# Gather, prefix sum and matmul: three engines' unrolled streams become loops of 16 tiles with waits on counted registers

## The chip, the cores and the metric

The kernel runs on one NeuronCore of a Trainium2 chip. The metric is the device time of one execution in microseconds (us), as a median over several executions. A core has TensorE (PE: matmuls, with its weight loads shown as PEld), VectorE (DVE), ScalarE (ACT), GpSimd (POOL) and SyncE (SP), each running its own stream of instructions in order, and 16 DMA engines that move data between the DRAM and the on-chip SBUF. Engines wait for each other by semaphores: counters that an instruction raises when it ends and that others wait on. PE writes into PSUM[...], which VectorE and ScalarE read.

## The reference

For each of 16 batches, 2048 rows of 512 floats are picked from 4096 by sorted indices, their running sum along the rows is taken, and the result is multiplied by a 512 x 512 matrix.

```python
def reference(x, indices, w):
    B, S, D = x.shape                      # 16, 4096, 512
    N = indices.shape[1]                   # 2048
    b_idx = np.arange(B)[:, None]
    gathered = x[b_idx, indices, :].copy()
    cs = np.cumsum(gathered, axis=1)
    return np.matmul(cs, w).astype(np.float32)
```

## The kernel before

The work is cut into T = 256 tiles of 128 gathered rows, 16 tiles (NT) to a batch; two tiles (R = 2) make a group, the unit of storing. A tile goes through these steps, each on its own engine:

- `gather` (line 126, GpSimd): an indirect DMA brings 128 rows of 2 KB into one of 16 slots (NG) of `g32`. The gather of tile t waits until the pair of tiles that had its slots is cast (line 119).
- `cast` (line 141, ScalarE): float32 to float16 into `g16`, for one tile or for a pair at once.
- `sums` (line 152, PE): four matmuls with a triangle of ones (`ut`, or `uq` in the first and last group) give the running sums inside a tile, transposed, in one of four PSUM buffers `pa` (NA).
- `carry` (lines 171 and 184, VectorE): adds the last column of the tile before, and writes float16 to `cst`; the first tile of a batch is only copied. It waits for the sums of its tile and for its own carry before.
- `project` (line 195, PE): four matmuls with `w16` into one of four PSUM buffers `pb` (NB). Except in the first and last group it needs the carries of both tiles of its group.
- `drain` (line 207, ScalarE): copies `pb` to the output buffer `ob`.
- `store` (lines 216 and 221, SyncE): one DMA of 512 KB for a group, two of 256 KB in the first and last.

The order is written out by hand, one long unrolled stream for each engine, and set by a plan that is made in Python:

- ScalarE's stream (line 342) has, for each tile u, the casts of the list `casts[u]` and then the drain of u. The list (lines 106 to 114) keeps casts `far` tiles ahead of the drain: `far` grows from 2 to FAR = 10 with u // 8 and shrinks at the end with (T - 1 - u) // 6. Casts come in pairs while `far` is over 4.
- PE's stream (lines 319 to 334) sets sums of later tiles ahead of the project of tile u by `lead`: it grows from 1 to LEAD = 4 with u // 8 and shrinks at the end with (T - 1 - u) // 6. Inside a group of four matmuls it waits ahead for what the next group of matmuls needs (lines 150 and 193).
- VectorE's stream is carry after carry, GpSimd's is gather after gather, SyncE's is store after store.

All waits go through `Lane.need(sem, value)` (line 21), which leaves out a wait for a value that the engine has already waited for. Values are constants, since every tile has its own place in the unrolled stream. Most waits ride on the instruction that follows; where an instruction needs more of them, a wait instruction of its own stands ahead of it.

Before the first tile, small index loads (`idx_first`, line 229) serve the gathers of tiles 0 to 3. SyncE then issues two of the four loads of w (line 238, ScalarE the other two) and then the two loads of all indices (line 240). VectorE turns the indices to float (line 298), PE transposes them (line 303), and VectorE writes them back as `idxg` (line 309), which gathers from tile 4 on wait for. PE runs matmuls on zeros to stay warm: `busy(9)` ahead of the transposes and `busy(12)` behind them (lines 291, 299, 306). VectorE and ScalarE cast w to float16 (lines 312 and 341).

## Time and profile before

| what | value |
|---|---|
| median of 9 runs | 351.09 us (350.52 to 352.36) |
| the profiled execution | 351.98 us |
| its span in the profile | 350.3 us |
| PE busy, instructions | 307.8 us (88%), 2071 matmuls |
| ScalarE busy | 264.2 us (75%), 408 |
| GpSimd busy | 244.0 us (70%), 266 |
| VectorE busy | 179.1 us (51%), 263 |
| DMA | 135.91 MB, mean 388 GB/s |

The span begins with the first instruction of the program and ends with the last; the rest of the execution's time lies around it. The profile has a page (busy times, 40 slices of the span, DMA queues, the chain of work that ended last, groups of instructions by line) and views of the trace: waits, instructions in order of time, sums by stage. In a row of a group, `L126 POOL DMA_INDIRECT g<-in_x_dram,idxg x252 | 238.5, 946 | ...` means: line 126, GpSimd, 252 instructions of that kind, 238.5 us busy, 946 ns for one, and behind the second bar the idle time of the engine just ahead of them and what ended it. In a row in order of time the first number is the start and the second the duration, both in us; the brackets hold the idle time before. Registers, branches and waits are not counted as busy. PE's matmuls overlap, and their ends are modelled, so its busy share says little on how close it is to its limit. Queue q0 carries the gathers, q1 the stores, q8 and q14 the instructions that the engines themselves fetch.

### The profile page before, as it was taken

The numbers are of one execution on the slowest core, as the hardware profiler recorded it, in microseconds if no ns is written. First come the engines' busy times: TensorE is split into PE (matmuls) and PEld (weight loads), VectorE is DVE, ScalarE is ACT, GpSimd is POOL, SyncE is SP. The second block draws the span as 40 slices with busy tenths as digits, with TensorE's granted clock in tenths as the row PEclk, the third lists the DMA queues.
The fourth block names the chain that finished last, engine by engine and source line by source line (L and its number), as shares of the span: only waits on it lengthen the run. The fifth ranks groups of instructions, "written<-read, shape, count | busy, mean of one in ns | idle before, by whom it ended". The sixth has DMA issues, their size and how long they took to land.

```text
span 350.3 us, 5668 instructions
## 1 busy us (share of the span) xinstructions
PE 307.8 (88%) x2071; PEld 154.6 (44%) x2071; DVE 179.1 (51%) x263; ACT 264.2 (75%) x408; POOL 244.0 (70%) x266
## 2 busy tenths in 40 slices
PE   5878888999988899898999989889898989988984
PEld 2334443554444444454444445444454445544431
DVE  1335554565544555464555545555555556654441
ACT  3358876987687788787777778777777878877883
POOL 6777777777777777777777777777777777777000
PEclk9999999999999999999999999999999999999998
DMA  7699999999999999999999999999999999999974
GB/s 236 197 325 343 382 395 405 384 392 410 412 407 401 412 408 413 415 411 415 412 416 415 412 414 411 414 412 415 414 412 415 413 414 411 415 416 414 416 314 185
DMA packets 40635, 135.91 MB, mean 388 GB/s; under 512 B 6816, under 2 KB 7072, under 8 KB 40608
## 3 DMA queue, kind: packets, MB, share of 16 engines
q0 software_dynamic: 20480, 67.13, 49.7%
q1 hardware_dynamic: 19568, 67.91, 48.2%
q10 hardware_dynamic: 560, 0.53, 0.5%
q8 instruction: 16, 0.26, 0.3%
q14 instruction: 11, 0.09, 0.1%
HBM read 68.42 MB, written 67.11 MB: 387 GB/s over the span
## 4 chain that ended last, share of the span: by engine, by line
POOL 40%; DMA 17%; issue 16%; PE 14%; ACT 10%; DVE 1%; SPq 0%; ACTq 0%
POOL g L126 40%; DMA g<-in_x_dram,idxg 16%; PE pb L195 9%; ACT g L141 7%; PE pa L152 3%; ACT ob L207 3%; PE pb L291 1%; DMA idx<-in_indices_dram 1%; DVE cst L184 1%; SPq L238 0%; PE pb L303 0%; DVE cst L171 0%; SPq L229 0%; ACTq L23 0%; DVE idxf L298 0%
## 5 line engine op out<-in xcount | busy, mean ns | idle before, releaser
L126 POOL DMA_INDIRECT g<-in_x_dram,idxg x252 | 238.5, 946 | 77.1 <-issue 72.2
L195 PE MATMUL pb<-w,cst 128*128 128x512 f16 x1024 | 262.5, 379 | 3.8 <-DVE cst L184 3.1
L184 DVE TENSOR_TENSOR cst<-pa,cst 128x512 f16<-128x512 f32 x240 | 166.1, 692 | 141.1 <-PE pa L152 141.0
L141 ACT CAST g<-g 128x1024 f16<-128x1024 f32 (+1 forms) x148 | 137.6, 931 | 54.5 <-DMA g<-in_x_dram,idxg 51.8
L207 ACT COPY ob<-pb 128x512 f32<-128x512 f32 x256 | 139.9, 585 | 24.8 <-PE pb L195 24.8
L152 PE MATMUL pa<-ut,g 128*128 128x128 f16 x1008 | 110.4, 220 | 30.6 <-ACT ob L207 20.0
L152 PEld LDWEIGHTS pa<-ut,g 128*128 128x128 f16 x1008 | 71.1, 98 | 113.7 <-ACT ob L207 45.4
L195 PEld LDWEIGHTS pb<-w,cst 128*128 128x128 f16 x1024 | 89.3, 98 | 66.5 <-DVE cst L184 3.8
L171 DVE CAST cst<-pa 128x512 f16<-128x512 f32 x16 | 11.1, 692 | 17.2 <-PE pa L152 17.2
L291 PE MATMUL pb<-zeros 128*128 128x512 f16 x21 | 9.3, 633 | 1.5 <-DVE zeros L295 1.5
L291 PEld LDWEIGHTS pb<-zeros 128*128 128x128 f16 x21 | 3.1, 150 | 6.2 <-issue 4.7
L126 POOL DMA_INDIRECT g<-in_x_dram,idx_first x4 | 4.0, 993 | 1.6 <-issue 0.9
L298 DVE CAST idxf<-idx 128x128 f32<-128x128 uint32 x2 | 0.5, 228 | 5.9 <-DMA idx<-in_indices_dram 5.8
L338 ACT ACT_TABLE_LOAD x1 | 1.3, 1283 | 2.5 <-issue 2.5
L303 PE MATMUL pb<-ident,idxf 128*128 128x128 f32 x2 | 0.7, 460 | 2.1 <-DVE idxf L298 2.1
L152 PEld LDWEIGHTS pa<-uq,g 128*128 128x128 f16 x16 | 1.3, 112 | 1.4 <-ACT g L141 0.6
L303 PEld LDWEIGHTS pb<-ident,idxf 128*128 128x128 f32 x2 | 0.4, 181 | 3.1 <-issue 3.0
L152 PE MATMUL pa<-uq,g 128*128 128x128 f16 x16 | 1.6, 238 | 0.1
L341 ACT CAST w<-w 128x512 f16<-128x512 f32 x2 | 1.1, 616 | 0.5 <-DMA w<-in_w_dram 0.5
L295 DVE MEMSET zeros<- 128x256 uint32 x1 | 0.3, 272 | 1.1 <-SPq L82 1.1
L312 DVE CAST w<-w 128x512 f16<-128x512 f32 x2 | 0.8, 419 | 0.0
L309 DVE CAST idxg<-pb 128x128 uint32<-128x128 f32 x2 | 0.6, 292 | 0.3 <-PE pb L303 0.3
(11 smaller groups left out, 2.1 us busy)
## 6 DMA issues: line engine op xcount, KB each, us to landing
out_dram<-ob SPq DMA_DIRECT2D x126, 512.0 KB, 7.5
g<-in_x_dram,idxg POOLq DMA_INDIRECT x252, 9.3
out_dram<-ob SPq DMA_DIRECT2D x4, 256.0 KB, 2.7
w<-in_w_dram ACTq DMA_DIRECT2D x2, 256.0 KB, 4.1
w<-in_w_dram SPq DMA_DIRECT2D x2, 256.0 KB, 3.6
idx<-in_indices_dram SPq DMA_DIRECT2D x2, 128.0 KB, 4.6
g<-in_x_dram,idx_first POOLq DMA_INDIRECT x4, 3.6
idx_first<-in_indices_dram ACTq DMA_DIRECT2D x1, 2.0 KB, 2.1
```

Source lines behind the costliest of these rows:

```text
L126: nc.gpsimd.indirect_dma_start(out=g32[g % (NG // R)][:, r, :], out_offset=None, in_=x_flat, in_offset=bass.IndirectOffsetOnAxis(ap=ap, ax ...
L141: nc.scalar.copy(out=g16[g % NH][:, r : r + n], in_=g32[g % (NG // R)][:, r : r + n]).then_inc(s_c, 1)
L152: mm = nc.tensor.matmul(out=pa[t % NA][:, c], lhsT=g16[g % NH][:, r, c * P : (c + 1) * P], rhs=uq[:] if g in PLAIN else ut[:], start=(c == 0),
L171: nc.vector.tensor_copy(out=dst, in_=src).then_inc(s_d, 1)
L184: nc.vector.tensor_tensor(out=dst, in0=src, in1=last, op=mybir.AluOpType.add).then_inc(s_d, 1)
L195: mm = nc.tensor.matmul(out=pb[u % NB][:], lhsT=cst[g % NC][:, c, j, :], rhs=w16[:, c, :], start=(c == 0), stop=(c == DC - 1),)
L207: nc.scalar.copy(out=ob[g % NO][:, j], in_=pb[u % NB][:]).then_inc(s_e, 1)
L291: nc.tensor.matmul(out=pb[NB - 1][:], lhsT=zeros[:, :P], rhs=zeros[:], start=True, stop=True)
L303: nc.tensor.transpose(out=pb[k % NB][:, :P], in_=idxf[:, k, :], identity=ident[:]).then_inc(s_pt, 1)
L312: nc.vector.tensor_copy(out=w16[:, c, :], in_=w32[:, c, :]).then_inc(s_wc, 1)
L338: nc.scalar.copy(out=spare[:], in_=zeros[:, :1])
L341: nc.scalar.copy(out=w16[:, c, :], in_=w32[:, c, :]).then_inc(s_wc, 1)
```

## The change

The middle of three streams becomes a loop whose body is 16 tiles (U = NT) with an engine register as the count.

- VectorE: tiles 0 to 15 and 240 to 255 stay unrolled; 14 passes in between. The register `first` holds the first tile of the pass.
- PE: the plan up to the project of tile 31 and behind that of tile 223 stays unrolled; 12 passes in between. The register counts groups; tile counts are R times the register.
- ScalarE: tiles 0 to 31 and 224 to 255 stay unrolled; 12 passes.

`need` gets a `base`: inside a loop it waits for base + value, where base is the register, and remembers per pass what was waited for. At the head of each pass that memory is cleared. GpSimd and SyncE stay unrolled.

For every pass to be the same, the plan must be steady inside the loops. `far` now grows with u // 4 and shrinks with (T - 1 - u) // 4, so that it is 10 from tile 32 to tile 223 (before: 64 to 207). `lead` now grows with (u + 2) // 4; its end is as it was. Assertions check that the plan repeats.

Two edits stand apart from the loops: SyncE's two loads of all indices go ahead of the loads of w, and `busy(12)` becomes `busy(7)`.

```diff
-    def need(self, sem, value):
-        if value > 0 and self.seen.get(sem.num, 0) < value:
-            self.eng.wait_ge(sem, value)
-            self.seen[sem.num] = value
+    def need(self, sem, value, base=None):
+
+        seen = self.seen if base is None else self.in_pass
+        if base is None and value <= 0 or sem.num in seen and seen[sem.num] >= value:
+            return
+        self.eng.wait_ge(sem, value if base is None else base + value if value else base)
+        seen[sem.num] = value
+
+    def new_pass(self):
+        self.in_pass = {}
...
+    U = NT
...
-        far = min(FAR, 2 + u // 8, 2 + (T - 1 - u) // 6)
+        far = min(FAR, 2 + u // 4, 2 + (T - 1 - u) // 4)
...
-    def cast(t, n):
+    def cast(t, n, first=None):
         g, r = divmod(t, R)
         for u in range(t, t + n):
-            act.need(s_g[u % NG], 16 * (u // NG + 1))
+            act.need(s_g[u % NG], 16 * (u // NG + 1), first)
...
-    def sums(t, u):
+    def sums(t, u, first=None):
         g, r = divmod(t, R)
-        pe.need(s_c, cast_by[t])
-        pe.need(s_d, t - NA + 1)
+        tiles = None if first is None else R * first
+        pe.need(s_c, cast_by[t] if first is None else cast_by[2 * U + t] - 2 * U // R, first)
+        pe.need(s_d, t - NA + 1, tiles)
         for c in range(DC):
             if c == 1 and u is not None:
-                pe.need(s_e, u - NB + 1)
+                pe.need(s_e, u - NB + 1, tiles)
...
-    for c in range(DC):
-        eng = (nc.sync, nc.scalar)[c % 2]
-        eng.dma_start(out=w32[:, c, :], in_=w[c * P : (c + 1) * P, :]).then_inc(s_w[c], 16)
     for k in range(KI):
         nc.sync.dma_start(
             out=idx64[:, k, :], in_=idx_rows[k * P : (k + 1) * P, :]
         ).then_inc(s_idx[k], 16)
+    for c in range(DC):
+        eng = (nc.sync, nc.scalar)[c % 2]
+        eng.dma_start(out=w32[:, c, :], in_=w[c * P : (c + 1) * P, :]).then_inc(s_w[c], 16)
...
-    busy(12)
+    busy(7)
...
-    for t in range(T):
+    for t in range(U):
+        carry(t)
+    with nc.vector.Fori(U, T - U, U) as first:
+        dve.new_pass()
+        for t in range(U):
+            carry(t, first)
+    for t in range(T - U, T):
         carry(t)
...
-        lead = min(LEAD, 1 + u // 8, 1 + (T - 1 - u) // 6)
+        lead = min(LEAD, 1 + (u + 2) // 4, 1 + (T - 1 - u) // 6)
...
+    head = order.index((False, 2 * U - 1)) + 1
+    tail = order.index((False, T - 2 * U - 1)) + 1
+    step = 2 * U
...
+    for i in range(head):
+        run(i)
+    with nc.tensor.Fori(2 * U // R, (T - 2 * U) // R, U // R) as first:
+        pe.new_pass()
+        for i in range(head, head + step):
+            run(i, first)
+    for i in range(tail, len(order)):
+        run(i)
...
+    for u in range(2 * U):
+        step(u)
+    with nc.scalar.Fori(2 * U, T - 2 * U, U) as first:
+        act.new_pass()
+        for u in range(U):
+            step(u, first)
+    for u in range(T - 2 * U, T):
+        step(u)
```

`carry`, `project` and `drain` take `first` in the same way. `run` on PE calls `sums` or `project` for an entry of the plan, `step` on ScalarE is the old loop body for one tile.

## The prediction

> **What bounds the kernel now.** I read the slices first, then the groups, the waits, single tiles, and last the chain's end. Slices (clock, DMA busy share, GB/s in 40 slices) and queues:

> ```profile
> DMA  7699999999999999999999999999999999999974
> GB/s 236 197 325 343 382 395 405 384 392 410 412 407 401 412 408 413 415 411 415 412 416 415 412 414 411 414 412 415 414 412 415 413 414 411 415 416 414 416 314 185
> ...
> q8 instruction: 16, 0.26, 0.3%
> q14 instruction: 11, 0.09, 0.1%
> ```

> From about 60 us to 330 us the DMA engines are full at some 413 GB/s. They are half empty only in the first 20 us and the last 20. Instruction code is 0.35 MB.

> ```profile
> L126 POOL DMA_INDIRECT g<-in_x_dram,idxg x252 | 238.5, 946 | 77.1 <-issue 72.2
> L195 PE MATMUL pb<-w,cst 128*128 128x512 f16 x1024 | 262.5, 379 | 3.8 <-DVE cst L184 3.1
> ```

> GpSimd spends 946 ns on a gather and 0.3 us before the next: one per 1.25 us, never held, the last issued at 322.6 us. At 0.5 MB per tile (0.25 gathered, 0.25 stored) that asks for 419 GB/s, a little over what is granted. So gathers fall behind: in the trace's landing records tile 96 lands 8.7 us after its issue, tile 188 12.0 us, tile 255 16.6 us (at 339.26). Landings from tile 96 to 188 are 118.2 us apart, 1.285 us per tile. PE's 88% is no bound: where it catches up (VectorE's tiles 40 to 48, 66.98 to 75.67 us) it does a tile in 1.086 us. Waits from 100 to 300 us agree; compute waits for landings, PE for ScalarE's drains:

> ```profile
> POOL g L126 <- issue: 46.3, 152, 0.3
> ACT g L141 <- DMA g<-in_x_dram,idxg: 42.3, 75, 1.1
> PEld pa L152 <- ACT ob L207: 41.9, 73, 1.3
> ```

> The start, in order of time, and the chain's end:

> ```profile
> 8.12 4.47 PE L291 MATMUL pb<-zeros 128*128 128x512 f16 x10
> 8.63 1.18 POOL L126 DMA_INDIRECT g<-in_x_dram,idxg  x1 [0.57 <-DVE idxg L309]
> ...
> 13.24 0.79 PE L152 MATMUL pa<-uq,g 128*128 128x128 f16 x8
> ...
> 16.35 0.35 SPq L216 DMA_DIRECT2D out_dram<-ob  x1
> ```

> ```profile
> 338.82 0.39 PE L152 MATMUL pa<-ut,g 128*128 128x128 f16 x4
> ...
> 342.98 0.62 ACT L141 CAST g<-g 128x512 f16<-128x512 f32 x1
> ```

> Tile 0 has landed at 8.2 us but its sums wait for PE's warm-up matmuls until 13.24; the first store leaves at 16.35. At the end the last gather has landed at 339.26, its cast starts 3.7 us later, and from 317.8 us on the chain holds PE and ScalarE only.

> **The change, part by part.** *Loops.* TensorE makes 12 passes, ScalarE 12, VectorE 14, so 11, 11 and 13 taken branches. A pass of the loop has 20.6 us at the pace of landings (16 x 1.285). PE's floor is 16 x 1.086 = 17.4, so it has 3.2 us to spare. Every wait inside takes a register sum first. Counting the waits that a pass needs: TensorE 41, ScalarE 40 (16 gathers, 16 projects, 8 stores), VectorE 31. The trace has no register instruction; the nearest row is the plain wait instruction: 51 ns on TensorE, 21 on VectorE, 17 to 38 on ScalarE. So 41 x 51 = 2.1 us, 40 x 38 = 1.5 us, 31 x 21 = 0.7 us per pass, if each sum is one instruction. The compare-and-branch seen at the start takes 174 ns on TensorE, 47 on VectorE, 33 on ScalarE. Even all in line, 2.1 + 0.05 + 0.17 = 2.3 us is under TensorE's 3.2; ScalarE needs (0.952 + 0.477 + 0.52) / 2 = 0.97 us per tile (starts of cast, drain and drain about 152 us), spare 16 x 0.31 = 5 us; VectorE 0.75 us per tile, spare over 8. I take 0.1 us for the loops. The cover is the late landings; without it TensorE's 2.3 us per pass would cost 12 x 2.3 = 28 us. Queued behind a waiting matmul are all later ones of PE; VectorE waits for their sums, ScalarE for their projects, SyncE's stores for ScalarE.

> *The code of a loop.* [...] The row: q8 moves 16 KB packets, the first at 27.8 us and then one per 20 us, which is one for each 256 PE instructions (16 tiles of 8 loads and 8 matmuls); each takes some 1.05 us of one DMA engine. q14's 8 KB packets of the other engines take 0.31. [...] TensorE's pass is 256 instructions and 41 sums, about 300[...]. By this the code traffic falls: 11 packets of TensorE less (some 0.2 MB, 0.4 us of all engines). The trace can't say which, for it has no backward branch. I take the second[...] at 0; the other is a rival.

> *Start.* The index loads go ahead of w on SyncE's queue: two issues of w, 0.93 us together, no longer precede them, so the indices, transposes and idxg come 0.9 us earlier. GpSimd's fifth gather is then bound by its own pace, 7.12 + 1.25 = 8.37 in place of 8.63: 0.26 us. Both of SyncE's w loads come 0.91 us later; ScalarE casts w from 4.50 to 5.64 and is idle until 8.24, so this is covered by 2.6 us; VectorE's w casts come after idxg as before, and the first project is later still. Five warm-up matmuls less are 5 x 0.427 = 2.1 us of PE. First sums 13.24 - 0.9 - 2.1 = 10.2, first store 13.3. With gathers alone the DMA moved 203 of 413 GB/s, so 3.0 us earlier fills 3.0 x 0.51 = 1.5 us of it.

> *Ramp.* Lead 2 comes at tile 2 (was 8), 4 at tile 10 (was 24). At lead 1 tiles took (30.13 - 16.33) / 8 = 1.72 us, afterwards 1.23. From 20 to 30 us 347 of 413 GB/s flowed, so at most 0.16 x 10 = 1.6 us more. But far reaches 10 at tile 32 (was 64): a drain then stands behind casts of tiles ten ahead, so by 60 us drains are again pinned some ten tiles behind landings, as they were (29 against 39). What was stored early counts only while the gather queue doesn't run empty. Start and ramp: 3.1 at most, 0 at least, I take half, 1.5.

> *Tail.* Far falls from 10 at tile 224 (was 208) and pairs of casts go on to tile 249 (was 243); leads stay. Casts issued further ahead of the sums break the chain drain-cast-sums of the last 30 us. The cast of tile 255 was 3.7 us behind its landing, of which one project-to-drain step, 1.0 us, must stay: at most 2.7 gained. Against it, drains stand 2 to 3 tiles later at tile 224 (drain 224 ended at 308.85; steady spacing, landing of 234 at 310.72 + 2.9, gives 313.6) and 31 more at 1.086 us from there end at 347.3 where 346.57 was; but PE is four tiles ahead of the drains there, 4.3 us. I take 1.0 gained, bounds 2.7 gained to 1.5 lost.

> Sum: 0.26 + 1.5 + 1.0 - 0.1 = 2.7 us. The profiled execution took 351.98, a span of 350.3 and 1.7 around it; it becomes 349.3. It lies 0.9 over the median 351.09, which becomes **348.5**.

> **Rivals.** *1. The ends give nothing*: early stores are paid back before 60 us, the tail evens out: 351. For it: drains are pinned ten behind landings in both. Against: the tail chain has no DMA in it.

> *2. Code is fetched anew in each pass.* [...] Of a late gather's 16 arrivals the last comes 7.9 us after the eighth, and no packet of q8 moves that last one by more than 0.25 us, so TensorE's fetches lie on an engine with up to 7.9 us in hand: 4 to 15 us lost, less the 2.7: near 357. [...]

> *3. TensorE's sequencer becomes the bound* (this ends on the slower side). Place: register sums ahead of matmuls in each pass. If each wait takes two instructions of 51 ns, in line with the matmuls, 4.2 + 0.2 = 4.4 us against 3.2 to spare: 12 x 1.2 = 14 us, less 2.7: 362; at 100 ns each 60 us. It decides from 3.2 us per pass on, some 60 such instructions. Against it: matmuls and loads follow each other at 27 ns per instruction in the trace (13.65 to 13.81 us), so 256 take 7 us and the sequencer can run ahead. [...] by the 51 ns row alone the sums are in line at 2.1 us and still fit.

> *4. Less code helps more*: if those packets did sit on the engine that lands last, up to 7.9 us of lag shrinks by half, 4 us less, with three quarters of the 2.7: near 345.

> **How the numbers follow.** Chances: forecast 0.44 (own range 346 to 350.3), rival 1 0.13, rival 2 0.17, rival 3 0.20, rival 4 0.06. Low 345 leaves out half of rival 4; high 363 the upper part of rivals 2 and 3, together under 0.2. 0.2% is 0.7 us, about what can be told from no change. Faster: 0.42 of the forecast and rival 4, 0.48. Same: 0.02 and 0.10 of rival 1, 0.12. Slower: rivals 2 and 3 and 0.03 of rival 1, 0.40.

> **What would show it.** Right: first sums near 10.2 and first store near 13.3; GpSimd still at 1.25 us and never held; q8 with five to seven packets; landings at 1.28 us per tile; the last cast within 3 us of its landing. Rival 2: over 25 packets in q8[...]. Rival 3: PE at over 1.28 us per tile through the middle, ScalarE waiting for PE, GpSimd held by ScalarE. The prediction fails if compute, not landings, sets the middle, or if the later drains of tiles 208 to 240 aren't made up.

## The result, and the profile after

The kernel after takes 353.51 us (352.25 to 354.51), the kernel before, run beside it, 351.11. The ratio is 1.0068, 95% interval [1.0055, 1.008]: 2.4 us slower, where 2.6 us faster was forecast. The profiled execution took 353.38 us with a span of 351.7, so 1.7 us lie around the span as before.

The page's slices, queues and two costliest groups of the kernel after:

```profile
PEclk9988899999999999999999999999999999999998
DMA  7889999999999999999999999999999999999973
GB/s 237 265 299 295 327 347 395 402 411 417 416 415 417 416 415 416 414 417 413 415 414 416 413 413 413 414 413 413 413 410 411 411 415 413 412 413 413 409 319 138
...
q8 instruction: 5, 0.08, 0.1%
q14 instruction: 6, 0.05, 0.0%
...
L137 POOL DMA_INDIRECT g<-in_x_dram,idxg x252 | 238.3, 945 | 76.8 <-issue 70.4
L208 PE MATMUL pb<-w,cst 128*128 128x512 f16 x1024 | 266.3, 383 | 0.8 <-DVE cst L196 0.8
```

Three things stand in these lines. The loops are really loops: TensorE fetches its code in 5 packets instead of 16, the other engines in 6 instead of 11. GpSimd is as free as before: 945 ns for a gather, and the idle time before it is its own issue. And the loss stands in slices 3 to 6, roughly 18 to 53 us: before, they moved 325 343 382 395 GB/s, now 299 295 327 347, while TensorE's granted clock shows 8 for 9 in the first three of them. From slice 8 on the kernel after moves as much as the kernel before or a little more.

The waits of the whole run, engine, line and releaser, then total us, count and longest:

```profile
POOL g L137 <- issue: 71.3, 234, 0.3
ACT g L152 <- DMA g<-in_x_dram,idxg: 57.1, 96, 1.3
PEld pa L164 <- ACT ob L220: 52.1, 87, 1.3
```

The steady part is bound as it was: ScalarE waits for landings, TensorE for ScalarE's drains. TensorE's own register sums and branches are in none of these waits.

**The start** came earlier than forecast. The timeline of the kernel after (start, length, instruction, and in brackets the idle time before it):

```profile
8.37 0.95 POOL L137 DMA_INDIRECT g<-in_x_dram,idxg  x1 [0.30 <-issue]
...
8.70 0.38 PE L164 MATMUL pa<-uq,g 128*128 128x128 f16 x4 [0.96 <-ACT g L152]
...
11.62 0.35 SPq L229 DMA_DIRECT2D out_dram<-ob  x1
```

The fifth gather leaves at 8.37 as worked out; the first sums run at 8.70 (10.2 forecast, 13.24 before), the first store leaves at 11.62 (13.3 forecast, 16.35 before). So the kernel is 4.7 us ahead when it begins to store. Some of this lies in which execution was profiled. In eight profiled executions with the old start the drain of tile 0 ends at 14.8 to 16.3 us, in eight with the new one at 11.6 to 12.5, which is 3.5 us earlier in the mean.

**The ramp** loses that and more. The timeline of the kernel after between the drains of tiles 2 and 4:

```profile
14.56 0.59 ACT L220 COPY ob<-pb 128x512 f32<-128x512 f32 x1 [1.35 <-PE pb L208]
...
15.04 0.62 ACT L152 CAST g<-g 128x512 f16<-128x512 f32 x1
15.71 0.23 PEld L164 LDWEIGHTS pa<-ut,g 128*128 128x128 f16 x4 [1.69 <-ACT g L152]
...
15.95 1.03 PE L208 MATMUL pb<-w,cst 128*128 128x512 f16 x4
...
17.01 0.59 ACT L220 COPY ob<-pb 128x512 f32<-128x512 f32 x1 [1.35 <-PE pb L208]
...
18.57 1.91 PE L208 MATMUL pb<-w,cst 128*128 128x512 f16 x4
```

Read it downwards: the drain of tile 2, then on ScalarE the cast of tile 5, then on TensorE the sums of tile 5, behind them the project of tile 3, then the drain of tile 3. Each begins about when the one above ends (they overlap by 0.1 to 0.2 us), and the next turn begins with that drain: 0.48 from drain to cast, 0.67 to the sums, 0.24 to the project, 1.06 to the drain, 2.45 us for one tile. In each turn TensorE's weight loads wait 1.69 us, its matmuls 1.20 and ScalarE 1.35. The code says why. The change sets `far = 2 + u // 4` and `lead = 1 + (u + 2) // 4`. At tiles 2, 3, 6, 7, 10 and 11 both are 2 + u // 4: TensorE's order puts the sums of tile u + far ahead of the project of tile u, and ScalarE's order puts the cast of tile u + far directly ahead of the drain of tile u. Before, with both slopes u // 8, far was always at least lead + 1, so one cast was in hand. The same tiles in the timeline of the kernel before:

```profile
19.16 0.59 ACT L207 COPY ob<-pb 128x512 f32<-128x512 f32 x1 [1.23 <-PE pb L195]
...
19.64 0.62 ACT L141 CAST g<-g 128x512 f16<-128x512 f32 x1
...
20.25 0.59 ACT L207 COPY ob<-pb 128x512 f32<-128x512 f32 x1
...
22.58 0.59 ACT L207 COPY ob<-pb 128x512 f32<-128x512 f32 x1 [1.23 <-PE pb L195]
```

Every second drain follows without waiting for the cast just ahead of it to go through TensorE, so drains came 2.33 and 1.09 us apart by turns.

The last line of the kernel after is a second cost. The four matmuls of one project took 1.91 us from 18.57 on, where a tile has 1.03. The windows show the clock there (columns after the engines: granted clock, DMA share, GB/s):

```profile
core 0: us, PE busy (x) PEld busy (x) DVE busy (x) ACT busy (x) POOL busy (x), PEclk, DMA share, GB/s
14.61:18.02 3.41, 1.26 (x8) 0.53 (x8) 0.69 (x1) 2.06 (x5) 2.79 (x3) 1.00 0.96 329
18.02:21.43 3.41, 3.26 (x14) 1.74 (x15) 1.17 (x2) 1.52 (x4) 2.50 (x4) 0.50 0.89 308
24.85:28.26 3.41, 1.32 (x9) 0.59 (x10) 0.69 (x1) 2.06 (x5) 2.61 (x3) 1.00 0.96 332
28.26:31.68 3.42, 3.42 (x15) 1.77 (x16) 1.39 (x2) 1.51 (x3) 2.69 (x3) 0.50 0.95 338
35.09:38.50 3.41, 1.26 (x8) 0.53 (x8) 0.69 (x1) 2.06 (x4) 2.50 (x4) 1.00 0.97 347
38.50:41.91 3.41, 3.16 (x14) 1.75 (x15) 1.07 (x2) 1.00 (x3) 2.71 (x3) 0.50 0.96 335
```

Three times TensorE ran at half its clock for 3.41 us, and in the 3.41 us ahead of each it was busy for 1.26 to 1.32, 37 to 39%, with no idle time over 1.6 us. The drains of tiles 4, 8 and 12 came 3.5, 3.5 and 3.9 us after the ones before them in place of 2.45. The half clock is some 1 us of each; at tile 12 a cast of two tiles (1.05 us for 0.62) adds 0.4.

From the first drain to that of tile 12 the kernel after took 30.1 us and the kernel before 18.7. So, as an estimate from these lines, some 3 of the 11.4 us lost are the half clock and the rest is the chain. No run here has the chain without the half clock.

Both together, by the ends of drains (us, read from the trace; all differences against the profiled execution of before, which lies 0.9 us over its median):

```
tile       0     4     8    12    16    24    32    64   100   200   255
before  16.3  23.2  30.1  35.0  41.0  52.4  64.1 106.9 153.1 282.1 346.6
after   11.6  21.1  31.1  41.7  47.5  56.9  66.5 108.2 153.7 283.7 346.5
```

4.7 us ahead at tile 0, 6.7 us behind at tile 12. The late drains are late stores, and stores are half of what the transfers carry. The windows of before and of after:

```profile
20.00:40.00 20.00, 16.28 (x112) 7.64 (x112) 10.18 (x16) 15.53 (x29) 15.12 (x16) 1.00 0.99 353
40.00:60.00 20.00, 16.73 (x117) 7.99 (x116) 10.28 (x16) 15.24 (x25) 15.13 (x16) 1.00 1.03 402
60.00:100.00 40.00, 36.86 (x260) 19.45 (x258) 22.53 (x33) 32.02 (x47) 30.26 (x32) 1.00 1.02 401
```

```profile
20.00:40.00 20.00, 12.85 (x72) 6.17 (x71) 6.82 (x10) 9.78 (x17) 15.13 (x17) 0.84 0.92 307
40.00:60.00 20.00, 19.40 (x136) 10.57 (x135) 11.16 (x17) 17.47 (x26) 15.13 (x17) 0.95 0.98 359
60.00:100.00 40.00, 37.11 (x261) 19.43 (x259) 22.43 (x33) 31.11 (x47) 30.26 (x33) 1.00 1.03 412
```

(353 - 307 + 402 - 359) GB/s x 20 us = 1.8 MB less; the early start had moved 0.7 MB more between 10 and 20 us. By 60 us the kernel before has moved 18.87 MB of gathers and stores and the kernel after 17.81: 1.06 MB, or 2.6 us at 413 GB/s. The gathers are level (10.99 MB in both); all that is missing are stores (6.82 MB for 7.89). Afterwards the gap closes, to 0.07 MB at 300 us, so missing bytes alone don't explain the later end.

**The end.** Compute ends at the same time as before (last drain 346.5 and 346.6), though the kernel after was behind at tile 200. The chains of the kernel before and of the kernel after, from 318 us on:

```profile
by line: PE pb L195 41.1%; ACT g L141 16.6%; PE pa L152 11.7%; ACT ob L207 9.2%; issue 6.4%; DVE cst L184 2.1%; ACTq L23 0.2%
by line: PE pb L208 66.4%; PE pa L164 14.5%; ACT ob L220 3.7%; DVE cst L196 2.2%; ACT g L152 1.7%; issue 0.7%; ACTq L26 0.1%
```

TensorE is four fifths of it, where it was half: the tail now runs at TensorE's own pace. What ends later is the last store. A transfer has 16 arrivals in the trace (in the kernel before, 252 of the 256 gathers show all 16 and the others 14 or 15). The last three arrivals of all stores came at 348.6 us, all three, in the kernel before, and at 348.7, 349.4 and 350.0 in the kernel after. The gathers show the same: of gather 246 the 14th arrival came 6.4 us after its issue and the last 17.1 (before: 11.1 and 15.6). As a mean of the gathers of tiles 112 to 254 the last of the 16 arrivals came 2.3 us behind the one ahead of it before, and 6.5 us after. One part of the transfers is behind the rest, and further behind than before. That the missing early work is caught up by the others and not by this part is an argument from these figures; no record names the part.

### The profile page after: what moved, and what is told of

It reads as the page before. It is cut to its first block, busy times and chain, and to the rows that moved or that the text cites. A ratio compares the mean times of both kernels' runs of the same rounds, so it can differ in the third digit from the quotient of the medians.

```text
span 351.7 us, 6498 instructions
## 1 busy us (share of the span) xinstructions
PE 306.4 (87%) x2066; PEld 157.0 (45%) x2066; DVE 179.2 (51%) x263; ACT 262.2 (75%) x399; POOL 243.8 (69%) x266
## 4 chain that ended last, share of the span: by engine, by line
POOL 34%; DMA 26%; PE 17%; issue 13%; ACT 8%; DVE 0%; ACTq 0%; SPq 0%; POOLq 0%
POOL g L137 34%; DMA g<-in_x_dram,idxg 24%; PE pb L208 13%; ACT g L152 6%; PE pa L164 4%; ACT ob L220 3%; DMA g<-in_x_dram,idx_first 1%; DMA idx_first<-in_indices_dram 1%; DVE cst L196 0%; ACTq L26 0%; SPq L424 0%; POOLq L26 0%; SPq L90 0%
## 5 line engine op out<-in xcount | busy, mean ns | idle before, releaser
L208 PE MATMUL pb<-w,cst 128*128 128x512 f16 x1024 | 266.3, 383 | 0.8 <-DVE cst L196 0.8
L152 ACT CAST g<-g 128x1024 f16<-128x1024 f32 (+1 forms) x139 | 136.0, 980 | 58.4 <-DMA g<-in_x_dram,idxg 57.1
L220 ACT COPY ob<-pb 128x512 f32<-128x512 f32 x256 | 138.4, 586 | 20.8 <-PE pb L208 20.8
L164 PE MATMUL pa<-ut,g 128*128 128x128 f16 x1008 | 113.6, 222 | 34.7 <-ACT ob L220 22.5
L164 PEld LDWEIGHTS pa<-ut,g 128*128 128x128 f16 x1008 | 73.9, 99 | 115.6 <-ACT ob L220 52.1
L208 PEld LDWEIGHTS pb<-w,cst 128*128 128x128 f16 x1024 | 90.6, 99 | 64.6 <-issue 3.6
L183 DVE CAST cst<-pa 128x512 f16<-128x512 f32 x16 | 11.1, 692 | 14.5 <-PE pa L164 14.5
L304 PE MATMUL pb<-zeros 128*128 128x512 f16 x16 | 5.2, 485 | 1.5 <-DVE zeros L308 1.5
L304 PEld LDWEIGHTS pb<-zeros 128*128 128x128 f16 x16 | 1.9, 123 | 4.0 <-issue 1.9
```

What stands on the lines that cost most here:

```text
L152: nc.scalar.copy(out=g16[g % NH][:, r : r + n], in_=g32[g % (NG // R)][:, r : r + n]).then_inc(s_c, 1)
L164: mm = nc.tensor.matmul(out=pa[t % NA][:, c], lhsT=g16[g % NH][:, r, c * P : (c + 1) * P], rhs=uq[:] if first is None and g in PLAIN else ...
L183: nc.vector.tensor_copy(out=dst, in_=src).then_inc(s_d, 1)
L208: mm = nc.tensor.matmul(out=pb[u % NB][:], lhsT=cst[g % NC][:, c, j, :], rhs=w16[:, c, :], start=(c == 0), stop=(c == DC - 1),)
L220: nc.scalar.copy(out=ob[g % NO][:, j], in_=pb[u % NB][:]).then_inc(s_e, 1)
L304: nc.tensor.matmul(out=pb[NB - 1][:], lhsT=zeros[:, :P], rhs=zeros[:], start=True, stop=True)
```

## The experiments

Ratios are against the kernel before, run beside each, with 95% intervals; 0.1% is 0.35 us. The theories: *R*, the ramp, as above; *L*, the loops themselves cost; *E*, only the transfers count, and the ends give nothing.

**Unrolled.** The kernel after, with the three loops written out.

```
-    with nc.vector.Fori(U, T - U, U) as first: ...
+    for t in range(T): carry(t)
     # likewise for TensorE's order and ScalarE's steps
```

> The changed kernel with its plan, its start and its tail, but with no loops: all three streams written out to the last tile, waits on constants. Theory R (the ramp costs, the loops are hidden): like the changed kernel, 353.5 us within 0.8. Theory L (the loops' register sums and branches cost): 348 to 350 us, as forecast without them.

352.63 us, ratio 1.0044 [1.0027, 1.006]. Most of the loss is there without any loop, as R has it (its time lies just under R's), and some 0.24% goes with the loops, though the two intervals overlap.

**The lead of before.** The kernel after with the sums' lead put back, so that it stays under far.

```
-        lead = min(LEAD, 1 + (u + 2) // 4, 1 + (T - 1 - u) // 6)
+        lead = min(LEAD, 1 + u // 8, 1 + (T - 1 - u) // 6)
```

> The changed kernel with loops, but PE's lead grows as before, 1 + u // 8, so that in the ramp casts stand at least one tile further ahead than sums. Theory R: the 2.45 us per tile of the ramp go away, 348 to 350 us. Theory L: still near 353.

351.91 us, 1.0028 [1.0016, 1.0041]. The windows:

```profile
20.00:40.00 20.00, 16.80 (x120) 8.58 (x121) 10.45 (x16) 14.14 (x23) 15.13 (x17) 1.00 0.98 346
```

TensorE is back at its full clock and at 16.8 busy us of 20 (12.85), the transfers at 346 GB/s (307). The chain is gone, and with it 1.4 us of the loss (1.0068 less 1.0028). That is short of R's 348 to 350 and under L's 353: the lead is the larger part of the loss, and the loops, priced below, are most of the rest.

**Casts further ahead.** The same from the other side: the lead of after, and one more cast.

```
-        far = min(FAR, 2 + u // 4, 2 + (T - 1 - u) // 4)
+        far = min(FAR, 3 + u // 4, 2 + (T - 1 - u) // 4)
```

> The changed kernel with loops and its own lead, but far starts at 3 in place of 2 (3 + u // 4), so casts are a tile further ahead of the same sums. Theory R says that lead must stay below far, whichever of the two is moved: 348 to 350.5 us, ramp at 1.3 us per tile or less. If a lead of 4 at tile 10 is bad in itself, or theory L holds: near 353.

352.23 us, 1.0029 [1.0012, 1.0046]. The time is that of the lead put back, but R's 350.5 and its pace of 1.3 us per tile were missed: from the drain of tile 4 to that of tile 12 a tile took 2.08 us. Another wait had come in place of the chain, in its timeline:

```profile
29.24 1.04 ACT L152 CAST g<-g 128x1024 f16<-128x1024 f32 x1 [3.45 <-DMA g<-in_x_dram,idxg]
...
30.34 0.61 PE L164 MATMUL pa<-ut,g 128*128 128x128 f16 x4 [3.50 <-ACT g L152]
```

A cast that runs further ahead waits here for its landing, and the drains behind it wait too; TensorE had half its clock from 28.9 to 35.7 us. So this run agrees with the chain, but the run with the lead put back is the one that shows it.

**Loops only.** The kernel before with loops: TensorE and ScalarE over tiles 64 to 207, VectorE over 16 to 239; start, ramp and tail untouched.

> The kernel before with its own start, ramp and tail, and loops alone: PE and ScalarE from tile 64 to 207 in 9 passes, VectorE from 16 to 239 in 14. Theory R: 351.1 us within 0.7; q8 falls from 16 packets to some 7. Theory L: 353 us or more.

352.17 us, 1.0034 [1.0019, 1.0049], between the two expectations. The loops cost 0.9 us by the medians and 1.2 by the ratio, with less code to fetch:

```profile
q8 instruction: 8, 0.13, 0.1%
q14 instruction: 7, 0.06, 0.0%
```

**Ramp only.** The kernel before with the two new slopes at the beginning, nothing else.

```
-        far = min(FAR, 2 + u // 8, 2 + (T - 1 - u) // 6)
+        far = min(FAR, 2 + u // 4, 2 + (T - 1 - u) // 6)
...
-        lead = min(LEAD, 1 + u // 8, 1 + (T - 1 - u) // 6)
+        lead = min(LEAD, 1 + (u + 2) // 4, 1 + (T - 1 - u) // 6)
```

> The kernel before with only the two slopes of the ramp changed: casts run 2 + u//4 ahead instead of 2 + u//8, sums 1 + (u+2)//4 instead of 1 + u//8; no loops, the old start, the old tail. Theory R (the sums now run exactly as far ahead as the casts are issued, so that cast, sums, projection and drain of one tile form one chain from about tile 2 to tile 14): 352.6 to 353.7, 1.4 to 2.5 us above before, rows of VectorE-free gaps 'PE L.. LDWEIGHTS pa' held 1.7 us by ScalarE and 2.4 us from one drain to the next early in the kernel. Theory of the prediction (the ramp saves up to 1.6 us): 349.5 to 351. Theory E (only the loops cost, the ramp's delay is swallowed by the stream of transfers): 351.2, within 0.3 us of before.

354.42 us, 1.0101 [1.0087, 1.0116]: 3.5 us, more than the whole change and more than R had given it. Its windows:

```profile
20.00:40.00 20.00, 13.28 (x71) 6.17 (x69) 6.91 (x10) 9.86 (x18) 15.11 (x16) 0.83 0.91 306
40.00:60.00 20.00, 17.81 (x118) 9.37 (x117) 9.88 (x15) 14.99 (x22) 14.39 (x16) 0.91 0.94 327
60.00:100.00 40.00, 38.47 (x276) 20.90 (x274) 24.00 (x35) 33.74 (x52) 30.25 (x33) 1.00 1.02 409
```

The chain and the half clock are those of the kernel after; with the old start the last half-clock stretch ends at 46.0 us instead of 41.9. Here GpSimd is held too (14.39 for 15.13 busy): the gather of tile 40 leaves at 54.8 instead of 53.9, since its buffer is cast too late. By 60 us 16.86 MB have moved, 2.0 less than before, and 1.24 are still missing at 300 us, 3.0 us at 413 GB/s. Here most of the loss is bytes that were never made up.

**Start only.** The lists ahead of the weights, 7 warm-up matmuls for 12.

```
-    busy(12)
+    busy(7)
     # and the loop over idx64 ahead of the loop over w32
```

> The kernel before with only the start changed: the lists of indices are loaded ahead of the weights, and TensorE's warm-up has 7 matmuls instead of 12; no loops, the old ramp and tail. First sums should stand near 8.7 us and the first store near 11.6 us in every theory (13.2 and 16.4 before). Theory R leaves the start innocent: 349.5 to 351.2, since stores begin some 4 us earlier and what the transfers can move is used from then on. The rival (the start is what costs: weights and lists later, TensorE's clock not raised by the shorter warm-up): 352 to 353. Theory E (the slowest of the 16 transfer engines sets the end, and it has enough queued from 16 us on either way): 351.2, within 0.3 us of before.

350.82 us, 0.9998 [0.999, 1.0006]: nothing. It is paid back. Against the run with the tail edit only (below), which is the kernel before up to its last 48 tiles, the drain of tile 16 ends at 36.7 us for 39.5, and that of tile 32 at 62.9 for 62.6. In 40 to 60 us it moves 383 GB/s where that one moves 402. By 60 us it has moved only 0.07 MB more. In its timeline the paying back is a wait: the cast at 47.3 us waits 1.2 us for its landing, and TensorE 2.5 us for the cast.

**Tail only.** Casts stay far ahead for longer at the end.

```
-        far = min(FAR, 2 + u // 8, 2 + (T - 1 - u) // 6)
+        far = min(FAR, 2 + u // 8, 2 + (T - 1 - u) // 4)
```

> The kernel before with only the tail's casts changed: they stay far ahead for longer, 2 + (255-u)//4 instead of 2 + (255-u)//6. The prediction put it at 1.0 us gained, bounds 2.7 gained and 1.5 lost: 350.2. Theory E (the last transfers of the slowest engine set the end): 351.2, within 0.3 us of before. The rival (two-tile casts near the end wait for the later of two tiles and hold drains): 351.6 to 352.7.

350.06 us, 0.9979 [0.997, 0.9989]: 0.7 us gained, the one part that does what it was forecast to do. The last window:

```profile
300.00:340.00 40.00, 37.83 (x267) 20.39 (x266) 21.56 (x33) 33.67 (x54) 17.73 (x19) 1.00 1.01 408
```

The kernel before moved 400 GB/s there. 8 GB/s x 40 us is 0.32 MB, 0.8 us at 413.

**Start, tail and the new casts without the new lead, no loops.** The kernel of the run with the lead of before, its loops written out.

> The kernel after without its loops and with the sums' lead of before (1 + u//8), so that casts run ahead of the sums again: new start, new slopes of the casts at both ends, old lead. Theory R: 350.3 to 351.3, as good as before or better, some 0.8 us below the same edit with loops (351.9), if the loops cost that by themselves. If the loops cost nothing when the sums' lead is repaired: 351.6 to 352.2.

350.77 us, 0.9996 [0.9987, 1.0005], as R and L together expected. With loops the same edit, the run with the lead of before, stood at 1.0028: 0.32% for the loops.

**Start and tail.** As above with the old slope of the casts at the beginning.

> The kernel before with the new start and the new tail, the old ramp and no loops. Start alone gave 0.0 and tail alone 0.8 us. If the parts add: 350.0. It also prices the cast slope at the ramp by itself, since the kernel with the new cast slope at both ends and the old lead took 350.8: 0.7 us if this one takes 350.0, nothing if it takes 350.8.

350.39 us, 0.9983 [0.9975, 0.9991]. The parts add (0.9998 and 0.9979 make 0.9977). The new slope of the casts by itself costs little, 0.13%, within the two intervals.

**One loop at a time.** The kernel of "loops only", with two engines of three written out.

> The kernel before with TensorE's loop alone, over tiles 64 to 207; VectorE and ScalarE are written out, start, ramp and tail are those of before. The three loops together cost 0.9 us in that place. If TensorE's branch and sums cost it (208 ns per branch and 324 sums of 32 ns, a little of it on the path): 351.5 to 352. If another engine's loop costs it: 350.9, within 0.3 us of before.

> The kernel before with ScalarE's loop alone, over tiles 64 to 207. If ScalarE's loop costs the 0.9 us (sums of 35 ns ahead of each wait for a gather and for a project delay casts, casts delay the freeing of gather buffers): 351.5 to 352. If another engine's loop costs it: 350.9, within 0.3 us of before.

> The kernel before with VectorE's loop alone, over tiles 16 to 239, as in the kernel after. If VectorE's loop costs the 0.9 us (sums and merged register operations of 40 ns ahead of the wait for the carry of the tile before, in a chain where every carry waits for the last): 351.5 to 352. If another engine's loop costs it: 350.9, within 0.3 us of before. If each loop costs a third, all three stand at 351.2.

TensorE 351.3 us, 1.0007 [0.9998, 1.0016]; ScalarE 351.27, 1.0016 [1.0004, 1.0029]; VectorE 351.39, 1.0006 [0.9997, 1.0015]. All lie near the 351.2 of the last case. None carries it alone; they add to 1.0029, for the 1.0034 of all three. For two of them nothing at all is within the interval.

**Waits doubled, longer passes, old ramp, longer tail: on a chip with slow transfers.** These fell on a chip where the kernel before takes 445.6 us, and where the transfers moved 308 GB/s from 60 to 300 us (in the run with doubled waits) instead of some 413. They say what the edits do there, not what they do above.

```
 loops only, waits doubled     -  self.eng.wait_ge(sem, ...)      + the same line twice
 loops only, 48-tile passes    -  U = NT                          +  U = 3 * NT
 start, tail and loops         (the kernel after with the old slopes u // 8 at the beginning)
 tail only, longer             -  2 + (T - 1 - u) // 4            +  2 + (T - 1 - u) // 3
```

> The kernel before with the three loops, every wait inside the loops made twice, each with its own register sum. If sums and waits cost the loops' 0.9 us: the cost doubles, ratio near 1.006 to 1.007, 353.0 to 353.5 where before is 351.1. If branches or the missing fetches cost it: 1.003 to 1.004, as with single waits (352.2).

> The kernel before with the three loops over tiles 64 to 207 in passes of 48 tiles: 3 passes in place of 9, so 2 taken branches per engine in place of 8, and code fetched once for 48 tiles in place of once for 16. If branches cost the 0.9 us: a quarter of it is left, ratio 1.001, 351.3. If sums and waits cost it: 1.003 to 1.004, 352.1. If the missing fetches cost it (nothing in the trace says why they would): in between, 351.6.

> The change with only its ramp put back: new start, new tail, three loops (TensorE's and ScalarE's over tiles 64 to 207), the old slopes of casts and sums at the beginning. If the parts add: start and tail 0.9983, loops 1.0034, together 1.0017, 351.7. If the ramp is the whole loss and the loops cost nothing beside the new start and tail: 350.4. If the loss stays at 353 to 353.5, the ramp isn't the step that failed.

> The kernel before with its tail's casts kept far ahead for still longer: 2 + (255-u)//3, where //4 gave 0.9979. If the gain comes from breaking the chain of drain, cast and sums at the end: as good or better, 349.6 to 350.2. If later drains begin to cost: 350.3 to 351.5.

In that order: 1.0317 [1.0236, 1.0399], 0.9967 [0.9921, 1.0013], 1.0006 [0.9963, 1.0049], 0.9974 [0.9935, 1.0013]. Only the first says something: loops with doubled waits cost 3% there, where those with single waits and longer passes cost nothing that can be told. The other three can't be told from no change. Two were repeated where transfers run at 413 GB/s.

**Waits doubled, again.**

> The kernel before with the three loops, every wait inside the loops made twice, each with its own register sum; the same edit took 1.032 times the time of before on a chip whose transfers moved 306 GB/s. With transfers at 413 GB/s the loops with single sums and waits took 1.0034. If sums and waits cost this: ratio 1.006 to 1.012. If branches or the missing fetches cost it: 1.003 to 1.004.

352.77 us, 1.0047 [1.0031, 1.0063]. In the trace only the waits had doubled: ScalarE has 432 wait instructions of their own for 144, TensorE 381 for 12, VectorE 467 for 243, but the register sums are as many as before (162, 243 and 224), since both waits share one; the expectation had taken them to double. If waits carried the whole cost of the loops, 1.0068 was due, a little over the interval; if they carried nothing, 1.0034, which is inside it. They may carry a part.

**The change with the old ramp.** New start, new tail, loops, old slopes at the beginning.

> The change with only its ramp put back: new start, new tail, three loops, the old slopes of casts and sums at the beginning. With transfers at 413 GB/s: if the parts add, start and tail 0.9983 and loops 1.0034 make 1.0017. If the ramp is the whole loss: 0.998. If the loss stays at 1.006 or more, the ramp isn't the step that failed.

351.16 us, 1.0000 [0.9991, 1.001]. Its windows:

```profile
20.00:40.00 20.00, 17.00 (x116) 7.94 (x116) 10.74 (x16) 15.45 (x29) 15.12 (x17) 1.00 1.00 357
40.00:60.00 20.00, 15.02 (x106) 7.46 (x107) 9.10 (x14) 14.38 (x24) 15.12 (x17) 1.00 1.00 379
```

No half clock, no slow stretch, and the time of the kernel before. The interval leaves out both 1.0017 and 0.998; the loops cost 0.17% here, by 1.0000 over 0.9983. So the change is made of three terms: start and tail 0.9983, with the loops 1.0000, with the ramp as well 1.0068. The ramp is 2.4 us in this place, all of the result; loops and tail cancel. (TensorE and ScalarE make 9 passes in this run and 12 in the kernel after, so the 0.68% holds three passes too, an estimated 0.06 to 0.11% by what 9 cost. Without loops the ramp is 0.61%, 1.0044 over 0.9983.)

The smallest edit beats both kernels: the kernel before with the longer tail, 350.06 us. The new start adds nothing to it.

## Why the prediction was wrong

*Ramp* is the step that failed. It took from the profile that lead 1 is slow (1.72 us per tile) and later leads fast (1.23), and concluded that an earlier lead can only gain, "at most 1.6 us more". The second reading was narrow: 1.23 holds for tiles 8 to 12 alone, while tiles 8 to 32 took 1.42 in the same profile. More than that, it read far and lead each by itself, as slopes, and did not write down the two numbers tile by tile. At tiles 2, 3, 6, 7, 10 and 11 they are equal, which makes a chain of ScalarE and TensorE with 2.45 us per tile. The bound "0 at least" of start and ramp was therefore no bound: the ramp alone lost 3.5 us, and 2.4 with the new start and the loops. The half clock is part of it and was not thought of. In the profile of before the clock is full from 13.6 us to the end of the work: TensorE was busy for 7.4 of 10 us in its slowest ramp slice from 20 us on.

*Start* had its mechanism right and its value wrong. The first sums stood at 8.7 us and not at 10.2: the transposes ended at 6.2 us instead of 8.3, where 0.9 us had been counted, and the warm-up matmuls that were left ran 0.22 us apart and not 0.43, since the clock was full from 4.4 us on (before: from 13.6). What this start is worth is nothing: rival 1's sentence, early stores are paid back before 60 us, is what the run with the start alone shows. In the kernel after it may not be worthless: the ramp costs 3.5 us with the old start, and 2.1 (1.0044 over 0.9983) with start and tail new.

*Tail* was forecast at 1.0 us, measured 0.7. The order of its argument held in the kernel after also: the drain of tile 240 was 1.5 us behind, that of tile 255 level, and the last cast is 2.7 us behind its landing, within the 3 us named.

*Loops* were put at 0.1 us and cost between 0.6 and 1.2: four pairs of kernels that differ in the loops alone give 0.24, 0.32, 0.34 and 0.17%. The step had counted more than there is: per pass the trace has 27 register sums of 32 ns on TensorE, 18 of 35 on ScalarE and 16 of 40 on VectorE, and a branch of 208, 45 and 56 ns, so 1.1 us on TensorE where 2.3 were allowed for and 3.2 to spare. Matmuls run on across TensorE's branch at 0.215 us spacing, so it is hidden. What the cost is stays open. It spreads over the engines, and it shows in the landings: between tiles 112 and 208 a line through them rises by 1.302 us per tile as a mean of five kernels with three loops (1.297 to 1.306), and by 1.293 in seven without loops (1.288 to 1.296), so 0.9 us over 96 tiles, one profiled execution each. In the five the last of a gather's 16 arrivals comes 3.9 to 6.5 us behind the one ahead of it, in the seven 1.4 to 3.9. The same GB/s flow, GpSimd isn't held, and the engines' rows hold nothing longer. Branches were not separated from sums: the run with 48-tile passes fell on the chip with slow transfers.

*The code of a loop*: the reading that was chosen, that the code of a pass is not fetched anew, is right; nothing in the profile of before had shown it, and it was the author's estimate. Between the packets at 76.3 and 317.6 us q8 moves none, over 11 taken branches of TensorE, and it has the 5 packets forecast (16 before), so a body of about 300 instructions was not fetched again. The run with 48-tile passes goes further: its body has 768 matmuls and loads and 75 sums, over three packets, and TensorE fetches nothing in its second and third pass. Rival 2 falls with this; its 4 to 15 us rested on the 1.05 us of a packet and on a count of packets per pass and their place among the 16 arrivals, neither of which was shown. Rival 3 falls with the 1.1 us per pass. So does rival 4 in its direction. The 15th arrival of a gather comes 7.0 to 7.9 us after issue (means of tiles 112 to 254) in the seven kernels with TensorE's loop and 8.7 to 12.8 in the nine without, so fewer packets go with earlier transfers that come second to last, but not with an earlier last one.

The time lay inside the range by luck, for a reason that none of the cases named. (The prediction's own terms add up to 348.4, not 348.5; nothing hangs on it.)

## What to carry to other kernels

Where one engine's order runs ahead by "lead" and another's feeds it "far" ahead, write both out tile by tile over the ramp and keep far above lead by at least one; equal values made the pipeline a chain here (2.45 us per tile). A larger far is not free either: it made a cast, and the drains behind it, wait 3.45 us for a landing. When transfers are the bound, price each stretch by the bytes that it doesn't move: the earlier start was paid back in a middle that is full anyway (0.9998), and a stall in the ramp need not be (3.0 of the 3.5 us of the ramp alone). Do one part of a composed change alone before believing the sum: here the tail, the part beside the point of the change, was the only one worth keeping.

## What was not expected of the hardware

And one part in 16 of the transfers lies far behind the rest: of gather 246 the last arrival came 3.5 us after the one ahead of it in the kernel before (15.6 and 12.1 us after issue) and 10.6 in the kernel after (17.1 and 6.5), so that what relieves the others does not end the kernel sooner.
